# Window attention's weights turned by 32x32 blocks and multiplied in bands of 32 rows, with the retention state framed by 512 tokens

## The chip, the cores and the metric

The kernel runs on one core of a Trainium2 chip. The core has five engines with queues of their own: TensorE (PE, with its weight loads PEld), VectorE (DVE), ScalarE (ACT), GpSimd (POOL) and SyncE (SP, which here issues nearly all DMA transfers). The metric is the time of one execution on the device, in microseconds (us); the figure for a kernel is the median of several runs.

## What is computed

One decoder layer on 2048 tokens of width 1024, all in float32. The input is normalised (RMS) and projected once to 2816 columns, which feed two groups of heads; both groups are gated by SiLU, joined, projected back and added to the input.

```python
h = rms_norm(x, norm_w)
rq, rk, rv, rg, sq, sk, sv, sg = split(h @ w_in)      # 256,256,512,512,512,128,128,512 columns
# A: retention, 4 heads (keys 64, values 128), rotary phases, decay gamma per head
state = gamma**C * state + (k * zeta).T @ v            # carried from chunk to chunk
ro = ((q @ k.T) * decay) @ v + (q * xi) @ state
ro = group_norm(ro) * ret_norm_w * silu(rg)
# B: window attention, 8 query heads on 2 key heads of 64, window of 128 keys
logits = rms_norm(q) @ rms_norm(k).T / 8 + bias[distance]
out = softmax([logits, sink])[..., :-1] @ v            # a learned sink per head in the denominator
so = out * silu(sg)
return x + concat(ro, so) @ w_out
```

## The kernel before

**Products.** The three big products of the input (W2: window columns and half of the retention values; W1: retention queries, keys and the rest of the values; W3: gates) and the output product (W4) are done as block products with seven multiplications in place of eight (m = 1 to 7, `STEPS`), each multiplication on operands that are split into a high and a low part (`split`, line 551), so that three fast passes make one float32 product. These are the matmuls named `acc<-w,x` in the profile: 128x128 weights and 512 columns (384 in W1). ScalarE makes the high parts, VectorE the low ones and the sums of blocks. `HELD` (line 62) is the number of split blocks of W1 that are kept for W3.

**Chunks.** Window attention and retention work on 16 chunks of 128 tokens (`NCH`). They run while the products W1 and W3 run, their TensorE work set between product matmuls.

**Window attention** (`window`, line 1129; `attend`, line 1283; `values`, line 1186). For a chunk, queries are scaled on VectorE (`qn`) and turned by DMA; keys are scaled on VectorE with the norm weights (`kn`, line 1299), turned on TensorE, and copied twice into `ks`, a strip of keys in which a chunk finds its own and the previous keys side by side. The logits are made in blocks of 32 queries: a block sees exactly 160 keys (its own 32 and the 128 before), so 32 matmuls of 64 rows, 32 weight columns and 160 moving columns run on eight tiles of the array. VectorE adds the bias and takes the row minimum of the negated logits (`lg`, `nm`). Of the five 32-key blocks the first and the last are half masked, one where the other is not, so VectorE folds them together by a minimum (label `either`, line 1378), leaving 128 columns. ScalarE takes the exponential with the sum of the row (`pm`, `den`). TensorE turns `pm`, four 128x128 transposes for each of two key heads (label `turn weights`, line 1408), ScalarE copies the turned weights out (`pT`), and GpSimd selects from them the part that belongs to the query block's own keys (`own`, line 1424).

`values` then takes two chunks at once: 16 matmuls of 128 rows with `pT` (values in `vn` and `vs`, the second shifted by 32 rows), and 16 of 64 rows with `own` and the differences `vd` of the values at the two ends of a block's keys, which VectorE subtracts; five DMA loads bring the values of a pair. The result of a chunk is one PSUM bank, copied by ScalarE (`so`) and stored. Denominators (line 1432 to 1442) are settled for each chunk: a subtraction, ScalarE's exponential of the sink, an addition and a reciprocal (`rden`).

**Retention** (`keys_of`, `update`, `retain`, from line 908) takes sub-chunks of 64 tokens. The state is carried by a multiplication with gamma^64 and an addition, two `scalar_tensor_tensor` for each sub-chunk (line 987). Keys carry the decay to the end of their sub-chunk, queries the decay from its beginning, and the mask of scores (`dmask`) a factor to undo the surplus.

**Gating** (`gate`, line 1448). The gated outputs are turned for W4 by DMA, or, for the retention group's chunks that are not in `TURNED["gated"]`, on TensorE with a copy by ScalarE.

**What sets the order.** A list scheduler in the kernel (`Program.emit`, line 173) runs through all operations when the program is written. Each has a cost on the engines that can do it, a due time in units of product matmul groups, and buffers that it needs. At each step the operation that can start first goes next, ties by due time; TensorE's small matmuls in tiles (the sets of `CUTS`: tiled in quarters, eighths and so on) are held back by `LATER` and drawn together by `CROWD` and `SOONER`, since a change of tiling costs time (`change`, line 106). Line 376's `Order` then fixes that order over all engines. SBUF tiles come from one pool of 93 (`CAP`), with a limit for each purpose (`SHARE`), and at most six PSUM banks of the eight go to purposes other than products (`"rest": 6`). The due times of chunk c are `WIN[0] + c * WIN[1]` for the window, `RET` for retention and `GATE` for gates (lines 1564 to 1568).

Of the kernel before, what the change touches and what calls it, by code (L numbers as in the profile page):

```python
# [39 lines left out]
P = 128  # L40
# [19 lines left out]
SHARE = {"x": 15, "raw": 38, "acc": 21, "wr": 20, "wh": 20, "att": 38, "ret": 16, "rin": 12, "gate": 10, "mix": 34, "norm": 7, "res": 6, "turned": 7, "first": 5, "block": 3, "rest": 6}  # L60

HELD = 2
FIRST_X, SPLIT_X = 2.5, 0.6
# [30 lines left out]
CUTS = {"quarters": 1, "eighths": 2, "columns": 3, "both": 3}  # L94

ENDS = {"both": 1}
# [5 lines left out]
LATER, CROWD, MOST, SOONER = 13.0, 1.5, 4, 20.0  # L102
SETTLED, INSIDE = 0.2, 0.3
# [219 lines left out]

TURNED = {"q": range(NCH), "qk": range(NCH), "weights": (), "gated": range(0, NCH, 2)}
EARLIER_Q, EARLIER_K, EARLIER_U, LATER_W = 2.0, 3.0, 0.0, -1.0
# [42 lines left out]
VALUES = {P: dma(256, 0.6), 96: dma(192, 0.6), 32: dma(64, 0.6)}  # L370
# [30 lines left out]
def layer(ctx, tc, xt, xfirst, xtok, nw, w_in, w_rn, qkw, sinks, biasg, rope, decays, dmask, gpow, w_out, out):  # L401
# [87 lines left out]
    wq = fixed([P, 2, HD], "wq")  # L489
    wqk = fixed([P, HD], "wqk")  # L490
# [4 lines left out]
    dec = fixed([P, 2, RH], "dec")  # L495
# [7 lines left out]
    rden_all = [fixed([P, AH], f"rden{c}") for c in range(NCH)]  # L503
# [378 lines left out]
    def retention(at):  # L882

        for t, r in ((0, rstd_all), (1, rsq_all)):
            op(
                {"V": (0.25, 0.33, True)},
                lambda e, t=t, r=r: e.tensor_tensor(
                    factors[t](), dec()[:, t : t + 1, :].to_broadcast([P, NCH, RH]),
                    r().unsqueeze(2).to_broadcast([P, NCH, RH]), ALU.mult,
                ),  # L890
                [dec, r], [factors[t]], at(0) - 9, label="factors",
            )
# [63 lines left out]
    def update(c, chunks, states, due):  # L956
# [21 lines left out]
        for k, u in steps:  # L978
            new, old, kv = hb("state"), states[-1], kvs[u]
            if old is None:  # L980
                op(
                    {"V": dve(256)}, lambda e, new=new, kv=kv: e.tensor_copy(new(), kv()[:, 0:256]), [kv], [new],
                    due + 0.2, label="state",
                )
            else:

                def go(e, new=new, kv=kv, old=old, k=k):
                    for pr in range(2):
                        s, o = slice(pr * P, (pr + 1) * P), (2 * k + pr) * P
                        e.scalar_tensor_tensor(  # L990
                            new()[:, s], old()[:, s], gp()[:, pr : pr + 1], kv()[:, o : o + P], op0=ALU.mult, op1=ALU.add
                        )

                op({"V": (0.62, 0.7, False)}, go, [kv, old, gp], [new], due + 0.2, label="state")
# [134 lines left out]
    def window(at):  # L1129
# [5 lines left out]
            lambda e: e.scalar_tensor_tensor(wqk(), wq()[:, 0, :], -(HD**-0.5), wq()[:, 1, :], op0=ALU.mult, op1=ALU.mult),  # L1135
# [19 lines left out]
        vds = []  # L1155
        for _ in range(2):
            d = kb("vd", "att")
            quarters = [Part(d, lambda t, r=r: t[r, :]) for r in QUARTERS]
            for part in quarters[1:3]:
                op({"G": (0.65, 0.75, True)}, lambda e, part=part: e.memset(part(), 0.0), [], [part], at(0) - 4, label="no vd", also=(d,))  # L1160
            vds.append((d, quarters))
        held = []
        for c in range(NCH):
# [6 lines left out]
            if c % 2:  # L1170
                values(c - 1, held, at(c), *vds[c // 2 % 2])
                held = []

    def values_from(c, rows, part, n, whole, name, due):


        first = c * P + rows
        source = [akv_dram[k] for k in range(-1, NCH) if first < (k + 2) * P and first + n + 96 > (k + 1) * P]
        at = akv_rows[first : first + n, 128:256]
        src = bass.AP(at.tensor, at.offset, [[512, n], [32 * 512, 4], [1, P]])  # L1180
        op(
            VALUES[n], lambda e: e.dma_start(part().rearrange("p (u d) -> p u d", d=P), src), source, [part], due - 4,
            label="load " + name, also=(whole,),
        )

    def values(c, held, due, d, differences):
# [3 lines left out]

        n, s = kb("vn", "att"), kb("vs", "att")

        last = QUARTERS[3]
        parts = [Part(n, lambda t: t), Part(s, lambda t: t[0:96, :]), Part(s, lambda t: t[last, :])]
        for k, t, rows, part, many in ((0, n, 0, parts[0], P), (1, s, 32, parts[1], 96), (1, s, 0, parts[2], 32)):
            values_from(c + k, rows, part, many, t, t.name, due)
        for k, place, of, rows, whole in ((0, differences[0], parts[0], QUARTERS[0], n), (1, differences[3], parts[2], last, s)):
            values_from(c + k, P, place, 32, d, "vd", due)
            op(
                both(512),  # L1200
                lambda e, place=place, rows=rows, whole=whole: e.tensor_tensor(place(), place(), whole()[rows, :], ALU.subtract),
                [place, of], [place], due + 1, label="vd", also=(d, whole),
            )


        pavs = [ps(), ps()]
        own = held[0][1]

        def go(e):
            by = "p (i u q) -> p i u q"  # L1210
            for k, whole in enumerate((n, s)):
                for u in range(4):
                    for g, r in enumerate((L, H)):
                        e.matmul(
                            pavs[k]()[r, :].rearrange(by, u=4, q=32)[:, :, u, :], whole()[:, u * P + g * 64 : u * P + g * 64 + 64],
                            held[k][0][g]().rearrange(by, u=4, q=32)[:, :, u, :],
                            start=(u == 0), stop=False, skip_group_check=True,
                        )
            for u in range(4):
                for g, r in enumerate((L, H)):  # L1220
                    for k, rows in enumerate((L, H)):
                        e.matmul(
                            pavs[k]()[r, :].rearrange(by, u=4, q=32)[:, :, u, :],
                            d()[rows, u * P + g * 64 : u * P + g * 64 + 64],
                            own[g]()[rows, :].rearrange(by, u=4, q=32)[:, :, u, :],
                            start=False, stop=True, skip_group_check=True,
                        )

        late = due + (LATER_W if c in TURNED["weights"] else 0)
        reads = [*parts, *differences, *held[0][0], *held[1][0], *held[0][2], *held[1][2]]  # L1230
        op(f32(512, 3.2), go, reads, pavs, late + 2, "both", label="values", also=(n, s, d, *own))
        for k in range(2):
            so = kb("so", "att")
            op({"A": act(512)}, lambda e, so=so, k=k: e.activation(so(), pavs[k](), AF.Copy), [pavs[k]], [so], late + 2.1,
               label="so")
            store(so_dram[c + k], so, late + 2.2)
# [45 lines left out]

# [387 lines left out]
```

## Time and profile before

| | |
|---|---|
| time, median of 3 runs | 687.02 us (686.66 to 690.02) |
| profiled execution, own time | 688.87 us |
| profiled execution, span from first to last instruction | 687.1 us |
| mean granted TensorE clock in the span | 0.995 |
| TensorE / VectorE / ScalarE / GpSimd busy | 679.3 / 604.5 / 481.5 / 43.1 us |
| DMA | 178.54 MB, mean 260 GB/s |

How the lines are read: every instruction is recorded with line 397 (the helper that puts it in order), so groups are told apart by the tile they write and the tiles they read, `out<-in`, with the shape and the count. "Busy" is the time in which at least one instruction of the group ran, the mean is that of one instruction from start to end, and pipelined instructions overlap. After the second bar stands the engine's idle time just before the group and what ended it. `m` is any PSUM bank that is not a product's. A float32 matmul leaves two records on PE, a transpose one. Window attention's first logits begin 172 us into the span; the last values are multiplied at about 451 us. The output product ends the span.

### The profile page before, as it was taken

How to read it: one execution, taken by the hardware profiler on the slowest of the kernel's cores; microseconds unless marked ns; L12 is line 12 of the kernel's file. 1: busy time of each engine (PE TensorE's matmuls, PEld its weight loads, DVE VectorE, ACT ScalarE, POOL GpSimd, SP SyncE). 2: the span in 40 equal slices, each digit the busy share in tenths (PEclk: the TensorE clock that was granted, in tenths of full speed). 3: DMA queues.
4: the chain of work that ended last, by engine and by line, in shares of the span. 5: the costliest groups of instructions: out<-in, count | busy, mean ns of one | idle time of the engine just before them, and what ended most of it. 6: DMA issues, size and time to landing. Idle time of an engine off the chain costs nothing.

```text
span 687.1 us, 15551 instructions
## 1 busy us (share of the span) xinstructions
PE 679.3 (99%) x5428; PEld 577.9 (84%) x5428; DVE 604.5 (88%) x1479; ACT 481.5 (70%) x1137; POOL 43.1 (6%) x75
## 2 busy tenths in 40 slices
PE   9999999999999999999999998999999999999998
PEld 7888888889999999998887786888888888888886
DVE  6999877778898979899999898898899899999962
ACT  7666965657795665979888899887999954254300
POOL 1000000025010000011010010000000000000000
PEclk9999999999999999999999998999999999999999
DMA  9999964999977699999999898589999996216722
GB/s 323 384 322 309 397 209 179 332 292 290 328 222 206 205 266 315 302 326 286 327 317 291 252 266 224 185 259 276 343 329 287 316 264 194 64 47 210 254 102 93
DMA packets 166175, 178.54 MB, mean 260 GB/s; under 512 B 70864, under 2 KB 99664, under 8 KB 166096
## 3 DMA queue, kind: packets, MB, share of 16 engines
q1 hardware_dynamic: 165952, 177.53, 84.9%
q8 instruction: 43, 0.70, 0.4%
q14 instruction: 36, 0.29, 0.1%
q10 hardware_dynamic: 144, 0.00, 0.0%
HBM read 106.12 MB, written 56.69 MB: 237 GB/s over the span
## 4 chain that ended last, share of the span: by engine, by line
PE 96%; ACT 2%; DVE 1%; DMA 1%; issue 0%; DVEq 0%; ACTq 0%
PE acc L397 83%; PE m L397 13%; ACT ro L397 1%; DMA ro_dram<-ro 1%; DVE lg L397 0%; ACT pm L397 0%; DVE sT L397 0%; DVE x L397 0%; DVE qn L397 0%; DVE tsin L397 0%; ACT w L397 0%; DVE tcos L397 0%; DVE w L397 0%; DVE qk L397 0%; DVE t L397 0%
## 5 line engine op out<-in xcount | busy, mean ns | idle before, releaser
L397 PE MATMUL acc<-w,x 128*128 128x512 f32 (+1 forms) x2700 | 593.0, 378 | 0.2 <-DVE x L397 0.2
L397 PEld LDWEIGHTS acc<-w,x 128*128 128x128 f32 x2700 | 493.8, 189 | 83.0 <-issue 3.3
L397 DVE TENSOR_TENSOR x<-x 128x512 fp32r<-128x512 f32 (+2 forms) x218 | 145.7, 690 | 9.4 <-ACT x L397 9.3
L397 ACT ACTIVATE x<-x 128x512 fp32r<-128x512 f32 (+1 forms) x185 | 109.7, 614 | 20.8 <-DVE x L397 16.7
L397 DVE TENSOR_TENSOR w<-w 128x512 fp32r<-128x512 f32 (+3 forms) x96 | 60.4, 653 | 3.2 <-ACT w L397 3.1
L397 ACT ACTIVATE w<-w 128x512 fp32r<-128x512 f32 (+1 forms) x72 | 40.9, 599 | 21.3 <-DVE w L397 9.6
L397 ACT ACTIVATE pm<-lg,nm 128x128 f32<-128x128 f32 x128 | 49.7, 393 | 3.8 <-DVE lg L397 2.8
L397 DVE CUSTOM_DVE_ANT_0 lg<-m,bias,nsnk 128x160 f32<-128x160 f32 x128 | 42.4, 378 | 9.6 <-PE m L397 7.1
L397 DVE SCALAR_TENSOR_TENSOR w<-w,nw_sb 128x512 fp32r<-128x512 f32 (+3 forms) x72 | 49.5, 706 | 1.3 <-ACT w L397 1.2
L397 DVE TENSOR_TENSOR s<-acc,s 128x512 f32<-128x512 f32 (+1 forms) x64 | 41.5, 648 | 8.6 <-PE acc L397 8.2
L397 POOL TENSOR_SCALAR_AFFINE_SELECT own<-pT 64x512 f32<-64x512 f32 x32 | 25.4, 806 | 232.6 <-ACT pT L397 222.6
L397 DVE TENSOR_TENSOR t<-acc,t 128x512 f32<-128x512 f32 (+2 forms) x33 | 21.1, 639 | 16.6 <-PE acc L397 16.4
L397 ACT ACTIVATE x<-go 128x512 fp32r<-128x512 f32 x40 | 24.1, 626 | 14.7 <-PE acc L397 4.4
L397 ACT ACTIVATE apart<-qn 128x1024 uint16<-128x1024 uint16 x16 | 16.7, 1054 | 20.1 <-DVE qn L397 20.0
L397 ACT ACTIVATE w<-w,nw_sb 128x512 fp32r<-128x512 f32 (+3 forms) x45 | 28.6, 678 | 2.0 <-DMA w<-in_w_in 2.0
L397 DVE TENSOR_TENSOR x<-go,x 128x512 fp32r<-128x512 f32 x40 | 27.0, 683 | 0.3 <-ACT x L397 0.2
L397 DVE TENSOR_TENSOR t<-acc,s 128x512 f32<-128x512 f32 (+1 forms) x32 | 20.8, 650 | 6.8 <-PE acc L397 6.7
L397 ACT ACTIVATE ro<-ro,nmu,rg 128x128 f32<-128x128 f32 x64 | 25.1, 481 | 0.0
L397 ACT ACTIVATE c<-acc 128x512 f32<-128x512 f32 (+1 forms) x24 | 13.4, 560 | 15.9 <-PE acc L397 14.2
L397 ACT ACTIVATION_READ_ACCUMULATOR pm<-lg,nm 128x1 f32 x128 | 24.4, 191 | 0.0
L397 ACT ACTIVATE s<-acc 128x512 f32<-128x512 f32 (+1 forms) x32 | 17.7, 564 | 9.5 <-PE acc L397 8.3
L397 DVE TENSOR_TENSOR r<-acc,t 128x512 f32<-128x512 f32 (+1 forms) x32 | 20.8, 651 | 3.5 <-PE acc L397 3.4
(132 smaller groups left out, 670.8 us busy)
## 6 DMA issues: line engine op xcount, KB each, us to landing
x<-in_xt SPq DMA_DIRECT2D x78, 256.0 KB, 4.9
x<-s_dram SPq DMA_DIRECT2D x64, 256.0 KB, 4.4
planes_dram<-apart SPq DMA_DIRECT2D x56, 256.0 KB, 4.5
w<-in_w_in SPq DMA_DIRECT2D x40, 256.0 KB, 5.4
s_dram<-x SPq DMA_DIRECT2D x32, 256.0 KB, 4.5
xk<-in_xtok SPq DMA_DIRECT2D x32, 256.0 KB, 5.2
res<-in_xtok SPq DMA_DIRECT2D x32, 256.0 KB, 4.0
w<-in_w_out SPq DMA_DIRECT2D x20, 256.0 KB, 4.6
```

Of the source, the lines that this page charges most:

```text
L397: return lambda *a, **k: self.order.put(op(*a, **k))
```

## The change

- `attend`: no fold of the first and last block, no transposes on TensorE, no `pT`, no select on GpSimd. The exponential runs over all 160 columns in place. VectorE transposes each 32x32 block of the weights (`transpose`, twice for each of four banks: 256 columns into `side`, 64 columns of the fifth block into `last`).
- `values`: for each chunk, 40 matmuls of 32 rows (one query block's 32 keys at a time, five key blocks in turn, on four row bands and two column halves), 128 moving columns, into four PSUM banks, one for each query block; two chunks are done together (`BANDED = 2`). The values come in by one DMA for each chunk (`values_of`), kept for the neighbour; no differences. The four banks are copied by ScalarE in four pieces for each chunk.
- Denominators are settled for four chunks at once (`settle`, `SETTLE = 4`).
- Key norms: ScalarE scales the keys (`kn`), and the norm weights go in with the copy of the turned keys (`ks`), as a scale for each partition.
- Retention: factors are taken relative to a frame of 512 tokens (`BASED = 4` chunks), so the state is only added to (one `tensor_tensor` of 256 columns for each sub-chunk), and ScalarE rescales it by gamma^512 at the end of each frame (three times).
- `HELD` is 3 in place of 2; nine chunks' gated outputs are turned by DMA in place of eight; the due times, the costs of drawing tiled work together and single chunks' due times (`WIN_BY`, `RET_BY`, `GATE_BY`) have new values.

```diff
-HELD = 2
-FIRST_X, SPLIT_X = 2.5, 0.6
+HELD = 3
+FIRST_X, SPLIT_X = 2.5, 0.4
-CUTS = {"quarters": 1, "eighths": 2, "columns": 3, "both": 3}
-ENDS = {"both": 1}
+CUTS = {"quarters": 1, "eighths": 2, "bands": 3}
+ENDS = {}
-LATER, CROWD, MOST, SOONER = 13.0, 1.5, 4, 20.0
-SETTLED, INSIDE = 0.2, 0.3
+LATER, CROWD, MOST, SOONER = 13.0, 2.0, 4, 10.0
+SETTLED, INSIDE = 0.15, 0.25
+BASED = 4
+SETTLE = 4
-TURNED = {"q": range(NCH), "qk": range(NCH), "weights": (), "gated": range(0, NCH, 2)}
-EARLIER_Q, EARLIER_K, EARLIER_U, LATER_W = 2.0, 3.0, 0.0, -1.0
+TURNED = {"q": range(NCH), "qk": range(NCH), "weights": (), "gated": (0, 2, 4, 6, 8, 9, 10, 12, 14)}
+EARLIER_Q, EARLIER_K, EARLIER_U, LATER_W = 0, 2.5, 2.5, -1.0
+BANDED, BANDS_DUE = 2, 1.5
...
-                def go(e, new=new, kv=kv, old=old, k=k):
-                    for pr in range(2):
-                        s, o = slice(pr * P, (pr + 1) * P), (2 * k + pr) * P
-                        e.scalar_tensor_tensor(
-                            new()[:, s], old()[:, s], gp()[:, pr : pr + 1], kv()[:, o : o + P], op0=ALU.mult, op1=ALU.add
-                        )
+                    lambda e, new=new, kv=kv, old=old, k=k: e.tensor_tensor(
+                        new(), old(), kv()[:, 2 * k * P : 2 * k * P + 256], ALU.add
+                    ),
+                if (2 * (c + k) + u) % (2 * BASED) == 2 * BASED - 1:
...
+                            e.activation(new()[:, s], new()[:, s], AF.Copy, scale=gp()[:, pr : pr + 1])
...
+    def values_of(c, due):
+        v, n = kb("vb", "att"), 4 if c < NCH else 1
+        source = [akv_dram[k] for k in range(c - 1, min(c + (n > 1), NCH))]
+        at = akv_rows[c * P : (c + 1) * P, 128:256]
+        src = bass.AP(at.tensor, at.offset, [[512, P], [32 * 512, n], [1, P]])
...
+            for k, (sides, lasts, o, _) in enumerate(held):
+                for j in range(5):
+                    for u, r in enumerate(QUARTERS):
+                        for g, to in enumerate((L, H)):
+                            v, at = (vs[c0 + k], j * P) if j < 4 else (vs[c0 + k + 1], 0)
+                            if j < 4:
+                                w = sides[g]()[r, :].rearrange("p (i k) -> p i k", k=P)[:, :, j * 32 : j * 32 + 32]
+                            else:
+                                w = lasts()[r, o + g * P : o + (g + 1) * P].rearrange(by, q=32)
+                            e.matmul(
+                                banks[u]()[to, k * P : (k + 1) * P].rearrange(by, q=32),
+                                v()[r, at + g * 64 : at + g * 64 + 64], w,
+                                start=j == 0, stop=j == 4, skip_group_check=True,
+                            )
...
+    def settle(i, nm, den, nms, dens, nsnk, due):
+        es, many = sb("es", [P, SETTLE, AH]), SETTLE * AH
...
-                e.scalar_tensor_tensor(
-                    kn()[:, g * HD : (g + 1) * HD], b()[:, g * HD : (g + 1) * HD], fac()[:, 8 + g : 9 + g],
-                    wqk(), op0=ALU.mult, op1=ALU.mult,
+                e.activation(
+                    kn()[:, g * HD : (g + 1) * HD], b()[:, g * HD : (g + 1) * HD], AF.Copy, scale=fac()[:, 8 + g : 9 + g]
                 )
...
-                pk()[:, 0:P].unsqueeze(1).to_broadcast([P, 2, P]), AF.Copy,
+                pk()[:, 0:P].unsqueeze(1).to_broadcast([P, 2, P]), AF.Copy, scale=wqk()[:, 0:1],
...
-                l4 = lg()[:, 0 : n * 160].rearrange("p (j b k) -> p j b k", j=n, b=5)
-                e.tensor_tensor(l4[:, :, x, :], l4[:, :, 0, :], l4[:, :, 4, :], ALU.min)
...
-                    for j in range(GRP):
-                        e.transpose(pp()[:, j * P : (j + 1) * P], pm()[:, j * P : (j + 1) * P], ident())
...
+                lambda e, of=of, most=most: e.transpose(most().rearrange("p (j k) -> p j k", j=2), of()[:, :, 0:P]),
...
+                lambda e, of=of, rest=rest: e.transpose(rest().rearrange("p (j k) -> p j k", j=2), of()[:, :, P:160]),
...
-WIN = (52.0, 5.3)
-RET = (109.0, 2.8)
-GATE = (143.0, 4.1)
-LEAD = 10.0
+WIN = (46.0, 5.25)
+RET = (109.0, 2.85)
+GATE = (140.0, 3.6)
+LEAD = 7.0
```

246 lines of the change are left out of this document (114 added, 132 removed).

## The prediction

> **What bounds the kernel now.** I read the page's busy times first, then its chain of waits, then the busy times by stage.
>
> ```profile
> PE 679.3 (99%) x5428; PEld 577.9 (84%) x5428; DVE 604.5 (88%) x1479; ACT 481.5 (70%) x1137; POOL 43.1 (6%) x75
> ...
> PE 96%; ACT 2%; DVE 1%; DMA 1%; issue 0%; DVEq 0%; ACTq 0%
> ```
>
> TensorE is busy for 99% of the span and owns 96% of the chain. I therefore price the change by the TensorE time that it frees, provided the others keep up in the stage concerned. A split of the span into four stretches shows that stage:
>
> ```profile
> core 0: us, PE busy (x) PEld busy (x) DVE busy (x) ACT busy (x) POOL busy (x), PEclk, DMA share, GB/s
> 172.00:452.00 280.00, 276.79 (x3337) 242.75 (x3339) 256.00 (x819) 229.52 (x639) 25.41 (x32) 0.99 0.93 269
> 452.00:554.00 102.00, 102.00 (x754) 83.94 (x747) 91.26 (x210) 93.00 (x170) 0.00 (x0) 1.00 1.05 302
> ```
>
> The window attention lives in the 280 us from 172 to 452. There VectorE is busy 256.0 us (91%), ScalarE 229.5 (82%) and DMA 0.93. These are the cover under which a shorter TensorE has to run: 24 us of VectorE idle time is not much.
>
> **TensorE, removed and added.** The TensorE part of the timeline holds one pair of chunks. Columns: start, length, what, records; an f32 product leaves two records, a transpose one.
>
> ```profile
> 253.80 1.09 PE L397 MATMUL m<-pT,vn 128*64 128x128 f32 x16
> 254.72 1.04 PE L397 MATMUL m<-pT,vs 128*64 128x128 f32 x16
> 255.70 1.10 PE L397 MATMUL m<-own,vd 64*64 64x128 f32 x32
> 256.73 1.34 PE L397 MATMUL m<-ks,qT 64*32 64x160 f32 x64
> 258.00 4.43 PE L397 MATMUL acc<-w,x 128*128 128x384 f32 x24
> 262.27 1.03 PE L397 MATMUL m<-ident,pm 128*128 128x128 f32 x8
> 263.06 1.82 PE L397 MATMUL acc<-w,x 128*128 128x384 f32 x9
> ```
>
> Matmuls overlap, so I count from start to start. The eight transposes of one chunk's weights take 263.06 - 262.27 = 0.79 us, 99 ns each. All 16 chunks lose them: 16 x 0.79 = 12.6 us. They stand between products on TensorE, so nothing hides them and their removal is worth its full length.
>
> The values of a pair take 256.73 - 253.80 = 2.93 us now. The new form issues 80 products, 160 records, each 32 rows deep, 64 wide and 128 columns long, on eight tiles. The trace has no such shape. The nearest row is the logits, also eight tiles: 64 records of 160 columns in 258.00 - 256.73 = 1.27 us, the change of tiling at the end included. By columns that gives 160/64 x 128/160 x 1.27 = 2.54 us, with the change of tiling counted twice. The 64*64 row has the right length, 128, on four tiles: 32 records in 1.03 us; at eight tiles half of 32 ns per record, 2.58 us. Counting one change of tiling (about 0.2) once, I take 2.43: saved 0.5 us a pair, 4.0 us in eight. Bounds: at best twice the tiles of the 64*64 row with no change of tiling, 2.1 us, saved 6.6; at worst four tiles at a time, 160 x 32 ns = 5.15 us, lost 17.8. I stay by the logits, which have the same number of tiles and the same f32 operands.
>
> One more gated chunk is turned by DMA: four transposes at 99 ns, 0.4 us saved.
>
> Weight loads are what could spoil this: 160 of them replace 64 per pair, all 64 columns wide. Two stretches of the load queue:
>
> ```profile
> 253.80 0.85 PEld L397 LDWEIGHTS m<-pT,vn 128*64 128x64 f32 x16 [0.25 <-issue]
> 340.73 0.61 PEld L397 LDWEIGHTS m<-qkT 64*64 64x64 f32 x32
> ```
>
> The first runs at 53 ns a load, but its products are 128 rows deep and set the pace themselves. The second, 64 columns wide too, runs at 19 ns, so loads to different tiles overlap. At 19 ns, 160 loads last 3.05 us, a bound of 8 x 0.62 = 5.0 us worse than my 2.43; that row is ended by its own change of tiling, so its inner pace is better. [...] This trace's 19 ns contradicts single file, and I go by the row.
>
> **The stall at the last chunk.** What ScalarE did meanwhile, TensorE's only long idle time, and the clock of the stretch after it:
>
> ```profile
> 423.18 2.25 ACT L397 ACTIVATE ro<-m 128x256 f32<-128x256 f32 x6
> ...
> 425.86 1.71 PE L397 MATMUL m<-ident,pm 128*128 128x128 f32 x6 [2.93 <-ACT pm L397]
> 426.00:432.00 6.00, 6.00 (x18) 4.73 (x19) 3.89 (x13) 5.97 (x19) 1.55 (x2) 0.51 0.36 131
> ```
>
> The transposes wait 2.93 us for an exponential that ScalarE has queued behind six copies of retention outputs; then the granted clock is 0.51 for 6 us, another 2.9 us. These 5.9 us belong to transposes that disappear. But the new values product waits, through VectorE, for the same exponentials, and it too has all later products queued behind it, with VectorE's additions waiting for those. I count half, 3.0 us; the range holds 0 and 5.9.
>
> **The other engines.** Groups of instructions, shapes kept apart (busy us, then mean ns):
>
> ```profile
> L397 ACT ACTIVATE pm<-lg,nm 128x128 f32<-128x128 f32 x128 | 49.7, 393 | 3.8 <-DVE lg L397 2.8 <-ACT ks L397 1.0
> L397 POOL TENSOR_SCALAR_AFFINE_SELECT own<-pT 64x512 f32<-64x512 f32 x32 | 25.4, 806 | 232.6 <-ACT pT L397 222.6 <-DMA a<-rq_dram 10.1
> L397 ACT ACTIVATE pT<-m 128x512 f32<-128x512 f32 x32 | 17.8, 587 | 0.5 <-PE m L397 0.2
> L397 DVE SCALAR_TENSOR_TENSOR state<-state,gp,m 128x128 f32<-128x128 f32 x60 | 17.7, 336 | 0.0
> L397 ACT ACTIVATE qk<-qk,factors 128x64 f32<-128x64 f32 x64 | 17.0, 338 | 8.7 <-DVE qk L397 8.7
> L397 DVE TENSOR_TENSOR lg<-lg 128x64 f32<-128x64 f32 x64 | 15.2, 243 | 0.0
> L397 ACT ACTIVATE ro<-m 64x256 f32<-64x256 f32 x32 | 12.1, 379 | 0.6
> L397 ACT ACTIVATE so<-m 128x512 f32<-128x512 f32 x16 | 8.6, 593 | 4.5 <-PE m L397 4.5
> L397 DVE SCALAR_TENSOR_TENSOR kn<-akv,fac,wqk 128x64 f32<-128x64 f32 x32 | 7.5, 273 | 0.0
> L397 DVE TENSOR_TENSOR sT<-m,dm 128x256 f32<-128x256 f32 x16 | 6.2, 416 | 0.9 <-PE m L397 0.8
> L397 DVE TENSOR_TENSOR vd<-vd,vn 32x512 f32<-32x512 f32 x8 | 5.9, 738 | 1.0 <-DMA vd<-aq_dram 1.0
> L397 DVE TENSOR_TENSOR vd<-vd,vs 32x512 f32<-32x512 f32 x8 | 5.5, 689 | 0.2
> L397 DVE TENSOR_TENSOR es<-den,es 128x8 f32<-128x8 f32 x16 | 3.4, 214 | 2.5 <-ACT es L397 2.5
> L397 DVE RECIPROCAL rden<-es 128x8 f32<-128x8 f32 x16 | 3.2, 203 | 0.5
> L397 DVE TENSOR_TENSOR es<-nm,nsnk 128x8 f32<-128x8 f32 x16 | 2.5, 158 | 0.0
> ```
>
> VectorE loses the minimum of outer blocks (15.2), the key norms (7.5), the value differences (11.4), three quarters of the three sink rows (9.1 to 2.3), and on the state 17.7 less 30 additions at the 416 ns of the 256-column row (12.5), so 5.2: 46.1 us in all. It gains 64 block transposes of 256 columns and 64 of 64. No row shows a DVE transpose. By the 256- and 64-column rows, 416 and 243 ns, they cost 64 x 0.659 = 42.2 us; bounds are half of that and double. Net -4 us, between -25 and +38. New is also that VectorE waits for ScalarE's exponential 64 times before a transpose, with the subtractions and bank-emptying additions behind it. The 16 waits for the sink's exponential cost 2.5 us, 0.16 each; 64 of them cost 10 us of idle time (bounds 0 and 20), which the 24 idle us cover. Without that cover they would go straight onto the path. GpSimd loses its 25.4 us of selects, off the path already.
>
> ScalarE loses 17.8 (transposed copies) and 8.6 (two value copies per pair). It gains 64 value copies of 128 columns, bounded by the 256-column row's 379 ns and half of it, at 0.28: 18; 32 key scalings at 17.0/64 = 0.27: 8.5; exponentials a quarter longer, 0 to 12, taken at 4; and rebasing with the extra DMA turn, about 3. Net +7, that is 237 of 263 us, 90%: tight, but TensorE can fill with products while one copy is late. The key norms now stand in ScalarE's queue, and the key's transpose and the chunk's logits wait for them; they are due before both, as VectorE's were.
>
> Settling denominators by fours makes the first three chunks of each group up to three chunks later. Rows of that tile (count, duration in ns, first to last start):
>
> ```profile
> L397 DVE RECIPROCAL rden<-es x16: 202/203/204, 178.9 to 427.3; 128x8 f32<-128x8 f32 x16
> L397 DVE TENSOR_TENSOR r<-r,rden x8: 679/682/684, 460.5 to 529.8; 128x512 f32<-128x512 f32 x8
> ```
>
> The last is made at 427.3 and the first used at 460.5, so this hides. The last group settles with chunk 15 as now; if the cover were gone, gating would slip by up to the wait itself. DMA: five loads of values per pair become about two (40 to 17 issues on SP's queue, some 1 MB less of 256 KB blocks), against one more turned chunk (a store and a transposing load) and one load less by the third held block. Moved this little, at 0.93 and with 1.05 reached in the next stretch, I cost it at 0. Values now hold four PSUM banks instead of two, so they can no longer sit beside the next logits under the limit of six banks: eight more changes of tiling in and out, 0 to 2 us (the load queue's 0.25 idle at such a change is the row), taken at 1.0.
>
> **Sum.** The profiled execution took 688.87 (span 687.1, the rest 1.8 around it), 1.85 above the median 687.02. 688.87 - 12.6 - 4.0 - 0.4 - 3.0 + 1.0 = 669.9; less 1.85 gives a median of 668.
>
> **Rivals.**
> - The neighbours absorb half. VectorE at 252 busy plus 10 of new waits fills the 263 us that TensorE now needs, and ScalarE stands at 90%. If every pair loses 1 us to such waits, 8 to 10 us return: 677. For it: the shared margin shrinks. Against: VectorE's work does not grow.
> - No gain. Block transposes at one and a half times the row's price add 21 us to VectorE: 252 + 21 + 10 = 283 of the old 280 us; or bands that run four at a time (+17.8 against -12.6). Either way some 687. Against: the price is by columns in every VectorE row, and the logits run eight tiles.
> - The order does not do what it says: the list of due times is new throughout, and other waits of the size of the 425.86 stall appear where transposes leave, three of them with their clock losses, 17.7 us: 686.
> - Slower: loads in single file. 160 x 53 ns = 8.5 us a pair, 5.6 more than now, 44.6 in eight, less 13: 719. It decides from 2.93 + 13.0/8 = 4.55 us a pair, 28 ns a load. For it is the 53 ns row, against it the 19 ns row.
>
> **Chances.** A measurement of this kernel tells 0.5% (3.4 us) from no change. Forecast 0.67, neighbours 0.16, no gain 0.05, order 0.05, slower 0.07 (loads in single file, or transposes at double price). Faster: 0.67 + 0.16 + a third of the two middle ones, 0.86; same 0.06; slower 0.08. The forecast alone spans 661 (whole stall gone, best bands, no extra tiling changes: 668 - 2.9 - 2.6 - 1) to 676 (stall stays, 19 ns loads: 668 + 3.0 + 5.0). To leave out no more than 2 in 10 I go to 659 and, past the neighbours' case, to 682.
>
> **What would show it.** The groups have no transposes of weights, no select, and 1280 band records at about 2.4 us a pair from start to start; single file would show 53 ns loads. VectorE's transposes near 416 and 243 ns confirm its sum; above 620 it becomes the bound, with TensorE idle behind it. The clock row after the last chunk stays near 1. The prediction is wrong if TensorE's idle time between 172 and 440 exceeds 10 us, or if the stretch is shortened by under 10 us.

## The result and the profile after

| | before | after |
|---|---|---|
| median, same chip, 20 runs each | 687.88 us (686.28 to 690.67) | 686.03 us (678.6 to 690.8) |
| profiled execution, own time | 688.87 us | 681.08 us |
| its span | 687.1 us | 679.3 us |

The ratio of after to before is 0.9945, with a 95% interval of 0.9929 to 0.9962; it leaves out the five slowest runs of after (688.9 us and more), and the two medians of the table, which hold them, differ by 0.3%. The change makes the kernel at most about half a per cent faster. The forecast was 668 us with a range of 659 to 682, so the median is outside the range and, by the ratio, some 15 us of the promised 19 are missing. The runs of the new kernel also spread over 12 us, where those of before spread over 4, and the quickest of them kept the clock highest (678.6 us at a mean granted clock of 0.997, 687.0 us at 0.990). The profiled execution is among the quicker ones. It is 7.8 us shorter than that of before, where the working promised 19, and what follows explains this difference; the 5 us by which the median run is slower still stand in no trace.

The page of after, its busy times, the instruction queue and the shares of the chain of waits:

```profile
span 679.3 us, 16734 instructions
...
PE 664.1 (98%) x6064; PEld 562.3 (83%) x6064; DVE 591.1 (87%) x1427; ACT 477.7 (70%) x1177; POOL 15.0 (2%) x39
...
q8 instruction: 48, 0.79, 0.5%
...
PE 98%; issue 2%; DVE 0%
```

TensorE did lose 15.2 us of busy time (679.3 before). But span less busy time, 7.8 us before, is now 15.2. In the chain of waits "issue" has grown from 0% to 2%: time in which TensorE waits for nothing that the profile shows. The list of what TensorE waited for (us in all, times, longest) says how often:

```profile
PE m L401 <- issue: 5.8, 3, 3.1
PE acc L401 <- issue: 4.9, 2, 2.5
PE m L401 <- DVE none L401: 1.2, 1, 1.2
```

Five waits, 10.7 us, none of them for another engine or a transfer. (The 1.2 us is the start of the program, and before has it too.) The wait of 2.93 us for ScalarE's exponential is gone. The stretch of the window attention, with the columns that were quoted for before:

```profile
core 0: us, PE busy (x) PEld busy (x) DVE busy (x) ACT busy (x) POOL busy (x), PEclk, DMA share, GB/s
172.00:452.00 280.00, 269.34 (x3937) 234.45 (x3936) 251.79 (x784) 230.11 (x680) 0.00 (x0) 0.99 0.99 276
```

TensorE idles for 10.7 of the 280 us, 3.2 before. VectorE and ScalarE are no busier than they were (251.8 and 230.1, against 256.0 and 229.5): they did not become the bound.

**Where the waits stand.** Four pieces of TensorE's timeline around them (start, length, what, records, idle time before and what ended it):

```profile
186.41 0.70 PE L401 MATMUL m<-side,vb 32*64 32x128 f32 x33 [1.45 <-issue]
...
272.00 1.01 PE L401 MATMUL m<-side,vb 32*64 32x128 f32 x50
274.22 0.36 PE L401 MATMUL m<-side,vb 32*64 32x128 f32 x7 [1.21 <-issue]
...
307.37 0.78 PE L401 MATMUL m<-ks,qT 64*32 64x160 f32 x32
310.55 3.64 PE L401 MATMUL acc<-w,x 128*128 128x384 f32 x20 [2.40 <-issue]
...
372.77 0.73 PE L401 MATMUL m<-ks,qT 64*32 64x160 f32 x19
376.62 0.50 PE L401 MATMUL m<-ks,qT 64*32 64x160 f32 x13 [3.12 <-issue]
```

Three of the five stops lie inside one operation, 19 records into the 32 of a logits group or 50 into a run of bands, where the profile shows no wait for an operand; the other two lie among a product's matmuls. What the five places have in common appears when TensorE's recorded instructions (6064 matmuls, 6064 weight loads, and 157 instructions for semaphores and the like that stand between them) are counted from the start of the program:

```
instructions   reached  since the previous  idle   resumed after the   16 KB packet of q8,
before it      at us    border, us          us     previous border     after the previous border
2241           184.69   4.16                1.7    5.9                 3.3 to 4.3
3009           209.94   1.99                2.9    4.9                 2.4 to 3.4
4801           272.74   1.89                1.5    3.4                 0.6 to 2.1
5825           308.07   2.25                2.5    4.7                 2.3 to 3.4
7873           373.20   2.16                3.4    5.6                 3.1 to 4.2
```

(Idle here is from the last start to the next, 0.1 to 0.4 us more than the profile's own idle time: 1.7 for 1.45 in the first row.) All five counts leave a remainder of 193 when divided by 256. Each time one packet of the queue that the profile calls "instruction" is on its way, and TensorE goes on 1.3 to 1.6 us after it has landed. (A border is the place between one group of 256 instructions, a page of code, and the next.) The queue moved 48 packets and 0.79 MB, 16 KB each; before it was 43 packets for 11,002 recorded TensorE instructions, now 48 for 12,285, that is 255.9 a packet in both. So in these two traces TensorE's code arrives in pages of 256 instructions, and it stops where it has executed one page before the next has come. Four of the five pages were run in 1.9 to 2.3 us, while the next one was there, and running, only 3.4 to 5.9 us after the previous border. The shortest page of before took 4.2 us and was left without a wait; but 4.2 us is no safe distance, as the first row of the table shows. That page of before:

```profile
363.00:367.20 4.20, 4.20 (x136) 3.54 (x128) 4.17 (x25) 3.68 (x19) 0.22 (x1) 1.00 1.07 370
```

One page of after for comparison, and the stretch of the wait behind it:

```profile
207.95:209.94 1.99, 1.99 (x144) 1.82 (x128) 1.99 (x5) 0.78 (x3) 0.00 (x0) 1.00 1.05 396
209.94:212.86 2.92, 0.45 (x6) 0.19 (x2) 0.67 (x2) 2.91 (x11) 0.00 (x0) 1.00 1.21 155
```

The page was run in 1.99 us, and the next one ran 4.9 us after the border before it.

What decides about a stop here is when the packet lands, not the length of the page alone. Counted in order, packets and pages match one to one (the first packet of a trace holds the page behind the second border), and the eleven traces of this case hold 504 such pairs. In 32 of them the packet had landed less than 1.2 us before TensorE reached the page, or landed later: TensorE then stood for 0.3 to 3.4 us from one start to the next, and every time it went on 1.28 to 1.62 us after the landing. In the other 472 it ran through, with 0.32 us from start to start at most. Before had one pair near the edge, at the end of the page shown above: landed 1.17 us ahead, 0.33 us from start to start. After has two quick pages that were followed by no stop, one of 2.2 us before 240.29 and one of 3.4 us before 305.82; their packets had landed 3.9 and 3.2 us ahead.

**The clock.** After the two longest waits the granted clock halves, to 0.53 and 0.51:

```profile
213.00:216.40 3.40, 3.40 (x12) 3.40 (x13) 1.76 (x3) 2.45 (x6) 0.00 (x0) 0.53 1.04 395
...
377.00:380.40 3.40, 3.40 (x14) 2.67 (x9) 3.21 (x18) 1.75 (x8) 0.00 (x0) 0.51 1.05 385
```

3.4 x 0.47 + 3.4 x 0.49 = 3.3 us. With the waits the new loss is 10.7 + 3.3 = 14.0 us. The account closes: TensorE's work without clock losses went from 679.3 - 2.9 = 676.4 to 664.1 - 3.3 = 660.8, that is -15.6; the stall at 425.86 with its clock went, -5.8; the code waits came, +14.0. Together -7.4, and the spans differ by -7.8.

**The parts of the change.** Groups of after, shapes kept apart:

```profile
L401 PE MATMUL m<-side,vb 32*64 32x128 f32 x1024 | 19.1, 274 | 2.7 <-issue 2.7
L401 DVE STREAM_TRANSPOSE side<-lg 128x256 f32<-128x256 f32 x64 | 27.6, 432 | 0.4 <-ACT lg L401 0.3
L401 DVE STREAM_TRANSPOSE last<-lg 128x64 f32<-128x64 f32 x64 | 13.5, 211 | 0.0
L401 DVE TENSOR_TENSOR state<-state,m 128x256 f32<-128x256 f32 x30 | 12.5, 416 | 1.9 <-PE m L401 1.7
L401 ACT ACTIVATE lg<-lg,nm 128x160 f32<-128x160 f32 x128 | 53.1, 420 | 4.6 <-DVE nm L401 4.6
L401 ACT ACTIVATE so<-m 128x128 f32<-128x128 f32 x64 | 11.6, 302 | 8.1 <-PE m L401 6.7 <-issue 1.3
L401 ACT ACTIVATE kn<-akv,fac 128x64 f32<-128x64 f32 x32 | 9.3, 346 | 1.4 <-DMA akv<-aq_dram 1.4
```

The transposes cost 432 and 211 ns (forecast 416 and 243), the state 12.5 us (12.5), the key scalings 9.3 (8.5), the longer exponentials 3.4 more (4). A pair of values that runs through (the border at 240.29 lies in it, and its packet had landed at 236.35):

```profile
238.51 1.19 PE L401 MATMUL m<-side,vb 32*64 32x128 f32 x63
...
240.98 3.22 PE L401 MATMUL acc<-w,x 128*128 128x384 f32 x17
```

240.98 - 238.51 = 2.47 us for 160 records, with 160 weight loads beside them. The working had 2.43.

### The profile page after: what moved, and what is told of

Same layout as the page of the kernel before. It is cut to its first block, busy times and chain, and to the rows that moved or that the text cites. A ratio compares the mean times of both kernels' runs of the same rounds, so it can differ in the third digit from the quotient of the medians.

```text
span 679.3 us, 16734 instructions
## 1 busy us (share of the span) xinstructions
PE 664.1 (98%) x6064; PEld 562.3 (83%) x6064; DVE 591.1 (87%) x1427; ACT 477.7 (70%) x1177; POOL 15.0 (2%) x39
## 4 chain that ended last, share of the span: by engine, by line
PE 98%; issue 2%; DVE 0%
PE acc L401 86%; PE m L401 11%; DVE t L401 0%; DVE none L401 0%
## 5 line engine op out<-in xcount | busy, mean ns | idle before, releaser
L401 DVE TENSOR_TENSOR x<-x 128x512 fp32r<-128x512 f32 (+2 forms) x217 | 143.2, 683 | 9.5 <-ACT x L401 8.7
L401 DVE TENSOR_TENSOR w<-w 128x512 fp32r<-128x512 f32 (+3 forms) x96 | 61.8, 671 | 0.1
L401 ACT ACTIVATE lg<-lg,nm 128x160 f32<-128x160 f32 x128 | 53.1, 420 | 4.6 <-DVE nm L401 4.6
L401 DVE STREAM_TRANSPOSE side<-lg 128x256 f32<-128x256 f32 x64 | 27.6, 432 | 0.4 <-ACT lg L401 0.3
L401 PE MATMUL m<-ks,qT 64*32 64x160 f32 x1024 | 23.0, 300 | 3.1 <-issue 3.1
L401 ACT ACTIVATE xk<-xk 128x512 f32<-128x512 f32 x32 | 19.8, 622 | 7.5 <-DMA xk<-in_xtok 7.5
L401 ACT ACTIVATION_READ_ACCUMULATOR lg<-lg,nm 128x1 f32 x128 | 24.6, 192 | 0.0
## 6 DMA issues: line engine op xcount, KB each, us to landing
x<-in_xt SPq DMA_DIRECT2D x77, 256.0 KB, 4.8
x<-s_dram SPq DMA_DIRECT2D x64, 256.0 KB, 5.2
planes_dram<-apart SPq DMA_DIRECT2D x57, 256.0 KB, 4.5
w<-in_w_in SPq DMA_DIRECT2D x40, 256.0 KB, 5.2
s_dram<-x SPq DMA_DIRECT2D x32, 256.0 KB, 4.9
xk<-in_xtok SPq DMA_DIRECT2D x32, 256.0 KB, 5.0
res<-in_xtok SPq DMA_DIRECT2D x32, 256.0 KB, 3.6
w<-in_w_out SPq DMA_DIRECT2D x20, 256.0 KB, 5.3
```

What stands on the lines that cost most here:

```text
L401: return lambda *a, **k: self.order.put(op(*a, **k))
```

## The experiments

**1. The same array time with fewer instructions.** The theory is the supply of code: the bands put 320 instructions (160 matmul records and 160 loads) into 2.47 us. The rivals are that the bands themselves are slow, or that something which the profile doesn't show (a bank, a transfer) holds TensorE. Here the four inner key blocks go through one matmul of 512 columns, so a pair needs 128 instructions for the same number of columns.

```diff
-                for j in range(5):
+                for j in (0, 4):
...
+                                e.matmul(
+                                    banks[u]()[to, :], vs[c0 + k]()[r, g * 64 : g * 64 + 64], sides[g]()[r, :],
+                                    start=True, stop=False, skip_group_check=True,
+                                )
```

> The changed kernel with the four inner key blocks of each band product put into one matmul of 512 columns in place of four of 128: the array streams as many columns, but a pair of chunks takes 128 TensorE instructions (weight loads included) in place of 320. It leaves out the right sums of window attention; order, waits, VectorE's, ScalarE's and DMA's work are untouched. Theory 'code' (TensorE runs out of instructions, which come in pages of 256, 16 KB each): the long stalls, 11 us in the trace of after, go with at most one left, the granted clock stays at 0.995 or above, the median falls from 686 to between 666 and 671, and the spread of runs shrinks from 12 us to under 5. Theory 'neighbours' (TensorE waits for results of VectorE or ScalarE that come late in the shorter stage): the stalls stay, 683 to 688.

Measured: 666.27 us (665.5 to 667.47), ratio to before 0.9689 (0.9672 to 0.9707). Its page, list of waits, and window attention's stretch:

```profile
span 664.4 us, 15198 instructions
...
PE 659.9 (99%) x5296; PEld 552.3 (83%) x5296; DVE 591.1 (89%) x1427; ACT 477.5 (72%) x1177; POOL 15.1 (2%) x39
...
q8 instruction: 42, 0.69, 0.4%
```

```profile
PE m L401 <- DVE none L401: 1.2, 1, 1.2
```

```profile
172.00:452.00 280.00, 280.00 (x3350) 236.50 (x3352) 263.50 (x819) 244.34 (x707) 0.00 (x0) 1.00 0.99 290
```

This kernel leaves out the adding up of the four key blocks, so it is an experiment and no cure. Every wait for issue is gone, TensorE is busy for all of the 280 us and the clock stays at 1.00. A pair takes 186.15 - 183.73 = 2.42 us from the first band to the next product, against 2.47, so the bands' own time is worth only 8 x 0.05 = 0.4 us of the 14.9 by which the span is shorter; 14.0 are the waits and the clock. VectorE (263.5) and ScalarE (244.3) carry the faster pace, which answers whether the neighbours could have: they can. The spread of the runs is 2 us again.

**2. The code moved by half a page.** 32 very small matmuls in the warm-up, 128 instructions, with nothing else changed.

```diff
             e.matmul(pw()[:, 0:256], none()[:, 0:P], none()[:, 0:256], start=True, stop=True)
+        for _ in range(32):
+            e.matmul(pw()[0:16, 0:2], none()[:, 0:16], none()[:, 0:2], start=True, stop=True)
```

> The changed kernel with 32 tiny matmuls (128 TensorE instructions) behind its warm-up, so that every page border of the code falls 128 instructions earlier in the work; the rest of the program and its order are the same. Theory 'code': the five stalls of after leave their places and others appear, again at one fixed remainder of the instruction count by 256; summed up over the trace's own instruction times, with 4.7 us from one border to the next at least, 14.2 us of stalls become 7.7. With 1.5 us for the tiny matmuls the median is 679 to 684. Theory 'neighbours': the stalls stay at the same instructions of the work, 686 to 689.

Measured: 680.05 us (675.83 to 683.33), ratio 0.9884 (0.9853 to 0.9916). TensorE's long waits are now at these places:

```
instructions before it   reached at us   remainder by 256
5057                     270.14          193
5825                     301.99          193
6849                     336.19          193
7873                     371.37          193
```

```profile
PE m L401 <- issue: 5.9, 3, 2.9
PE m L401 <- DVE none L401: 1.2, 1, 1.2
PE acc L401 <- issue: 0.8, 1, 0.8
```

The longest of them, at 336.19, is followed by halved clock (0.50):

```profile
339.57:342.98 3.41, 3.41 (x48) 2.61 (x33) 1.13 (x2) 1.57 (x8) 0.00 (x0) 0.50 1.30 339
```

The operations and their operands are the same, but the stops have moved to other operations, and the remainder has stayed. The work that stopped at 209.94 runs through here. A wait for data would have stayed with its operation. That the total is smaller (6.7 us of waits and 1.7 us of clock, 8.4 where after had 14.0) is where the borders happened to fall. By the two ratios, half a page of code that does nothing makes this kernel 0.6% faster, although the small matmuls themselves take some 2 us.

**3. More code in the kernel before.** Each logits matmul cut in two halves of 80 columns, which adds 128 instructions to every chunk, with the weights and values of before.

```diff
-                            e.matmul(
-                                pls[2 * t + g]()[q, j * 160 : j * 160 + 160], qT()[r, o : o + 32],
...
+                            for h in (0, 80):
+                                at = slot * 256 + u * 32 + h
+                                e.matmul(
+                                    pls[2 * t + g]()[q, j * 160 + h : j * 160 + h + 80], qT()[r, o : o + 32],
```

> The kernel before, with each logits matmul of 160 columns split into two of 80: the same columns and the same result, twice the instructions (256 in place of 128 for a chunk). Theory 'code': stalls appear in the kernel before too, 15 to 23 us by its own instruction times at 4.0 to 4.7 us a page, some with clock losses: 700 to 715. Theory 'neighbours': 687 to 690.

Measured: 704.23 us (702.98 to 707.57), ratio 1.0247 (1.0222 to 1.0273). The logits group, first in before, then in this kernel with its instruction queue and TensorE's waits:

```profile
L397 PE MATMUL m<-ks,qT 64*32 64x160 f32 x1024 | 22.3, 300 | 0.0
```

```profile
q8 instruction: 51, 0.84, 0.5%
...
L397 PE MATMUL m<-ks,qT 64*32 64x80 f32 x2048 | 35.7, 234 | 5.5 <-issue 5.5
...
PE m L397 <- issue: 6.1, 7, 1.7
```

The kernel without any bands now stops seven times, each time at a remainder of 193, six times in logits and once in a product of the retention. So the stops do not belong to bands or to VectorE's transposes, but to many instructions in a short time. The expected time was met partly by luck: 15 to 23 us of stalls were expected, some with clock losses, and 6.1 us came, with no halved clock. The rest of the loss is another price of an instruction: 2048 records of 80 columns are busy for 35.7 us where 1024 of 160 took 22.3. Half the columns did not halve a matmul's time; a chunk's 128 records take 205.03 - 203.03 = 2.00 us, 16 ns each. Account of the span: 13.4 + 6.1, less 1.7 by which the wait for `pm` is shorter, less 2.9 of clock, gives 14.9, and 702.0 - 687.1 is 14.9.

**4. An order that knows the borders.** If code is the cause, the order can be written so that the tiled operations do not crowd within a page. In this kernel the values are two operations, one for each chunk, and the list scheduler counts TensorE's instructions and lets no page be finished sooner than 5 us after the last.

```diff
+PAGE, FETCHED, FIRST_END = 256, 5.0, 193
...
+            page = (issued - FIRST_END) // PAGE + 1
+            b = FIRST_END + page * PAGE
+            if issued <= b < issued + n:
+                s = max(s, turned[-1] + FETCHED - occ * (b - issued) / n)
```

> The changed kernel with the values of a pair as two operations of one chunk each, and a planner that counts TensorE's instructions and lets a tiled operation start only when the next page of 256 is 5.0 us old by its reckoning, products going first. Theory 'code': nearly no long stall, more changes of tiling (1 to 3 us), median 667 to 673. Theory 'neighbours': no better than after, 684 to 690.

Measured: 685.29 us (682.05 to 688.98), ratio 0.9962 (0.9942 to 0.9981), a miss, and inside the range that was expected of the rival "neighbours". The trace tells the two apart: eight waits for issue remained, 8.1 us in all, each of them at a remainder of 193; the longest, 3.0 us, has 3.4 us of halved clock behind it. Two of the eight follow pages of 5.9 and 6.0 us, so 5 us were not enough here. The scheduler counts matmuls and loads; the program also holds 142 instructions for semaphores on TensorE, which are set in later, so the borders that it reckoned with drifted away from the real ones. That this is why the cure failed was not tested by itself.

**5. to 8. Spacing without borders.** The next rule, with the values still in two operations, needs no position: a tiled operation may end only when the last 256 TensorE instructions, wherever they begin, have taken at least `SPACED` us. It differs in that number alone: 5.0, 6.5, 4.0 and 4.5.

```diff
+CODE, SPACED = 256, 5.0
...
+        def spaced(o, s):
+            first = counts[-1] + codes(o) - CODE
+            if first <= 0 or o.set not in CUTS:
+                return s
+            i = bisect.bisect(counts, first)
+            part = (first - counts[i - 1]) / (counts[i] - counts[i - 1])
+            return max(s, times[i - 1] + part * (times[i] - times[i - 1]) + SPACED - o.cost["T"][0])
```

> The changed kernel with the values of a pair as two operations of one chunk each, and a planner that lets a tiled operation end only when the last 256 TensorE instructions up to its end took 5.0 us or more by its reckoning, wherever the page borders lie (the planner of e4 placed the borders without the semaphore instructions that the compiler adds, 142 of them, and so in the wrong places). Theory 'code': waits at page borders fall from 10 us to under 4, some 10 more changes of tiling cost 2 to 4 us, median 668 to 675. Theory 'neighbours' (now expected only if the shorter intervals between tiled operations starve VectorE): 680 to 688.

> As e5 with 6.5 us in place of 5.0, since single fetches in the traces took up to 7.1 us from one border to the next. Theory 'code': almost no waits at borders and runs closer together than in e5, but more changes of tiling and later window and retention work, 668 to 678. Theory 'neighbours': 682 to 690.

> As e5 (674.2) with 4.0 us in place of 5.0. Theory 'code': fewer changes of tiling and less delay of window and retention work than e5, but the slower fetches (4.3 to 7.1 us) make TensorE wait at borders again: one to four such waits of about 1 us, 670 to 678, with a wider spread of runs than e5's 2.7 us. Theory 'neighbours': no waits at borders.

> As e5 (674.2) with 4.5 us in place of 5.0. Theory 'code': between e5 and e7, at most two waits at borders, 669 to 677.

```
SPACED   time, us (runs)               ratio to before              waits at borders   shortest page, us
5.0      674.22 (673.66 to 676.34)     0.9797 (0.9771 to 0.9823)    none               5.2
6.5      687.21 (685.56 to 691.04)     0.9991 (0.9974 to 1.0009)    none               6.0
4.0      680.72 (677.88 to 681.69)     0.9899 (0.9882 to 0.9917)    1, 1.0 us          4.3
4.5      681.23 (680.13 to 684.28)     0.9920 (0.9900 to 0.9941)    2, 2.3 us          4.5
```

The waits at 5.0, and then the four longest at 6.5:

```profile
PE m L425 <- DVE sT L425: 1.8, 1, 1.8
PE m L425 <- DMA qT<-planes_dram: 1.5, 1, 1.5
...
PE acc L425 <- DVE nm L425: 0.9, 1, 0.9
PE acc L425 <- DVE r L425: 0.7, 1, 0.7
```

```profile
PE acc L425 <- DVE x L425: 2.2, 2, 1.3
PE acc L425 <- ACT x L425: 1.6, 1, 1.6
PE m L425 <- ACT so L425: 1.5, 1, 1.5
PE m L425 <- DVE sT L425: 1.3, 1, 1.3
```

At 5.0 the stops are gone, and what remains are four ordinary waits of 4.9 us in all. This kernel does all of the work and beats both the kernel before (by 2.0%, 1.8 to 2.3) and the change as it came. At 6.5 there are no stops at borders either, but the tiled work is held back so long that TensorE waits for its neighbours instead (8.8 us between 172 and 452, and 6.8 us of halved clock in the midst of four such waits between 381 and 391 us). The expectation of 668 to 678 us was missed, and the time lies where the rival "neighbours" had it; the trace agrees with that rival here, since its waits are for the neighbours. At 4.0 and 4.5 I expected less loss than was measured, and both expectations were missed (670 to 678 and 669 to 677 us). Waits at borders are back there, 1.0 and 2.3 us; the others are waits for neighbours and one of 1.5 us for issue away from any border (at 390.08, for 4.5), most of them between 386 and 398 us, and 3.4 us of halved clock at 4.5. So in these four traces the waits at borders are gone where the spacing is at least 5 us, as the theory says; but every new order also shifts other waits by some us, and the four times are not a curve of the spacing.

**9. The side parts alone.** The kernel before with the framed retention state and the key norms on ScalarE, with nothing done to weights and values.

```diff
+                op(
+                    {"V": dve(256)},
+                    lambda e, new=new, kv=kv, old=old, k=k: e.tensor_tensor(
+                        new(), old(), kv()[:, 2 * k * P : 2 * k * P + 256], ALU.add
+                    ),
...
+        op({"A": (0.47, 0.57, False)}, go, [b, facs], [kn], due, label="kn")
```

> The kernel before with two parts of the change alone: the retention state framed by 512 tokens and the key norms on ScalarE. They free about 12 us of VectorE and add some 9 us to ScalarE, and touch no TensorE instruction. If TensorE's own work and code set the time, nothing is gained: 684 to 690, the difference being the newly planned order's. If VectorE's load were what the stage waits for, 678 to 683.

Measured: 686.72 us (685.47 to 687.6), ratio 0.9989 (0.9978 to 1.0). VectorE's busy time falls from 604.5 to 592.6 us and nothing comes of it. TensorE's, 678.8 us, is nearly what it was (679.3), although the long wait and the 2.9 us of clock behind it are gone in this order; what took their place inside the busy time is not shown.

## Why the prediction was wrong

- **TensorE's work: right.** The working took 12.6 + 4.0 + 0.4 - 1.0 = 16.0 us off; TensorE's busy time without clock losses fell by 15.6. The bands ran at 2.47 us a pair (2.43), by the logits' row, and the loads to different tiles overlapped as the 19 ns row said: in the pair at 238.51, 160 loads of 0.13 us each took 2.30 us from the first start to the last end, 14 ns a load. Loads in single file, the slower rival at 53 ns a load, did not happen.
- **The stall at 425.86: too cautious.** I counted half of 5.9 us. All of it went: no wait for an exponential is in the list of after, and the clock there is 1.00.
- **The neighbours: right in the main.** VectorE's transposes came to 41.1 us (42.2), and 0.4 us of waiting stands before them, where I had 10. In experiment 1 both neighbours sustained a TensorE without any idle time (busy for 280.00 of the 280 us), so neither "the neighbours absorb half" nor "no gain" by slow transposes was at work. VectorE's busy time fell by 13.4 us where I had 4, and ScalarE's by 3.8 us where I had added 7, the latter mainly because the 64 value copies took 11.6 us and not 18.
- **The step that failed** is the one from TensorE time freed to time gained. The first paragraph prices the change "by the TensorE time that it frees, provided the others keep up", and the transposes' removal "is worth its full length" because nothing hides them. The proviso names the other engines and leaves out TensorE's own supply of instructions. The bands were priced by their columns and weighed against their weight loads, but the 192 more instructions in the values of a pair (320 for 128) appear in no term. The runs put 10.7 us of waits and 3.3 us of halved clock in that place, 14.0 us; with them gone the same chain of reasoning arrives at 666.3 us in experiment 1, where the forecast was 668 (and would have been 665 with the whole stall counted).
- **The rivals.** The third, "The order does not do what it says", named three waits with clock losses, 17.7 us together, and 686 us: near the measured time, but by luck, for a cause that was not there. "No gain" gave 687 and came as near, but neither of its conditions held: the transposes kept to the row's price, and the bands did not run four at a time (2.47 us a pair, against the 5.15 of that bound). The stops are at fixed counts of instructions and move when code is put ahead of them (experiment 2); no operand was late.
- **The warning that held.** The prediction was to be wrong "if TensorE's idle time between 172 and 440 exceeds 10 us": it was 10.7 us, and the views named there, which I had meant for VectorE's transposes, showed the new kind of wait at once. The other sign, a stretch shortened by under 10 us, tells little: the last values run at 418 us where they ran at 451, since the new order sets them earlier, while the span is 7.8 us shorter.
- **What was on the page before.** 43 packets in the instruction queue and 11,002 recorded instructions already gave 256 a packet. No wait of before gave a price for a late page, but the density could have been compared: 136 matmul and 128 load records in the densest 4.2 us of before, against 320 in 2.4 us in the forecast itself.

**Open.** The time from one border until TensorE ran on the next page varied from 3.4 to 5.9 us in these five waits. The packet took about 1.0 to 1.5 us of it and the way from landing to running 1.3 to 1.6; the variable part is the time before it starts, 0.6 to 3.3 us. Over all eleven traces a packet starts between 4.7 us before and 7.7 us after the previous border, and what sets it off is not shown. DMA is busy for 0.99 of this stretch, so queueing behind data is possible, but an experiment with fewer transfers at those moments wasn't tried. The spread of after's runs fits with a fetch of varying length; only the profiled execution shows where it was lost. Experiment 1 changes the count of instructions and of loads together, and the semaphore instructions on TensorE (154 in after) were not moved by themselves.

## What to carry to other kernels

When small tiled matmuls replace a few large ones, count instructions for each microsecond as well as columns, and compare them with the densest stretch of the trace that runs without a stop (here 256 in 4.2 us, with hardly anything to spare). No spacing was shown to be safe: the kernel spaced by 5 us had no wait at a border, but in other orders pages of 5.2 to 6.0 us were followed by stops of 0.6 to 1.6 us from start to start. In these traces, idle time that the profile puts down to issue, and that stands each time at the same remainder of TensorE's instruction count (193 by 256, semaphore instructions counted) with a packet of the instruction queue that is on its way or has landed less than 1.2 us ahead, was code that had not come; issue alone is not enough, as the wait at 390.08 for a spacing of 4.5 shows. Padding by half a page told it apart from a wait for data in experiment 2. What worked are fewer and longer instructions (0.969, in a kernel that leaves out some sums) and sparse instructions between dense ones (0.980, with all of the work); making the neighbours faster gave nothing (0.999).

## What the runs showed of the hardware that was not expected

- TensorE was stopped by its code: pages of 256 instructions, run in 1.9 to 2.3 us (one in 4.2), were followed by 1.5 to 3.4 us until the next page ran. In the eleven traces a stop at a border came only where the page's packet had landed less than 1.2 us ahead, and it ended 1.28 to 1.62 us after the landing.
- 160 records of 32-row bands with 160 weight loads ran in 2.47 us, 15 ns a record; matmuls of 80 columns took 16 ns a record too, so that halving the columns of the logits and doubling their number made them 1.6 times as long (35.7 us for 22.3).
- Of the five waits in the table, those of 2.9 and 3.4 us were each followed by 3.4 us at half the clock; the one of 2.5 us was not. At a spacing of 6.5 no wait in TensorE's list was over 1.6 us, and waits of 1.3, 0.8, 1.6 and 1.3 us between 381 and 391 us had 6.8 us at half the clock among them, from 387.5 on.
- VectorE's transpose of 32x32 blocks in float32 took 432 ns for 256 columns and 211 ns for 64 (with start and end), close to an addition of the same width (416 ns).
